# One level of Strassen's recursion on one row chunk in four of the gate and up projections

## The chip, the cores and the metric

The kernel runs on one NeuronCore of a Trainium2 chip. The core has a matrix engine (TensorE, PE in the profile), a vector engine (VectorE, DVE), a scalar engine (ScalarE, ACT), GpSimd (POOL) and a queue engine that issues loads (SyncE, SP). They run at the same time, each through its own list of instructions in order, and meet through semaphores. SBUF is the working memory with 128 partitions; PSUM holds eight banks of 128 x 512 fp32 numbers that only TensorE's products fill. The metric is the device time of one execution in microseconds.

## The reference

Two transformer blocks follow each other: one with an RWKV-7 branch and a softmax branch and a gated feed-forward part, and one with two kinds of attention. The change touches the feed-forward part of the first:

```python
    gate, up = jnp.split(_rms(h, n2) @ w_gu, 2, axis=-1)
    return h + (jax.nn.silu(gate) * up) @ w_dn
```

`h` has 256 rows that matter (plus 16 that are dropped at the end), the model width is 2048, and `gate` and `up` have 5632 columns each. So `w_gu` is a matrix of 2048 x 11264, all in fp32.

## The kernel before

**Precision by halves.** The products are made in the format fp32r, and each operand is split in two halves for it: `split` (lines 219 to 221) makes `hi` on ScalarE, a cast, and `lo = x - hi` on VectorE. `mm3` (line 270) multiplies with three matmuls, `hi hi + hi lo + lo hi`, into one PSUM bank.

**A weight chunk** is 256 rows by 512 columns of a matrix, held as 128 x 1024 numbers, 512 KB. `wload` (line 225) takes a raw buffer (three called `raw`, three called `raw2`, in turn), issues the load on SP's queue, and splits it into `hi` and `lo`, of which there are three buffers each. It does so with a raised priority, so that the order of the instructions has the loads and splits of later chunks ahead of the other work.

**A projection.** `gemm_b` (line 286) multiplies the 256 rows of activations by a column of chunks. Two banks of the four called `g` gather the two halves of the rows (`t` 0 and 1); for each chunk there are 2 x 2 x 3 = 12 matmuls, 128 x 512 each.

**The feed-forward stage** (lines 1008 to 1042). The 5632 hidden columns are 11 blocks of 512, in two groups (6 and 5). In each block `n`, `gemm_b` makes the gate from 8 chunks; ScalarE takes `tanh` of it (line 1028) and VectorE works on it (line 1029), both straight from the banks; `gemm_b` makes `up` from 8 more chunks, and VectorE multiplies (line 1032). Then `nat_to_t` (line 928) transposes the 256 x 512 result on TensorE, through the banks called `q` and `f`, and splits it into `hi` and `lo` for the next product. After each group the product with `w_dn` follows. A block has 16 chunks, 192 matmuls and 8 transposes.

**What sets the order.** From this stage on, a scheduler orders the instructions of all engines when the program is built, from the priorities and its own estimate of the times. On the chip each engine goes through its list as it stands: an instruction that waits holds back all that stands behind it on that engine, ready or not.

The functions that the change touches, with the line numbers of the profile:

## Time and profile before

| | |
|---|---|
| three runs | 2029.84, 2032.22 (median), 2036.05 us |
| the profiled execution | 2035.52 us, span 2033.8 us from its first to its last instruction |
| granted TensorE clock, mean | 0.989 |
| loads of `w_gu` | 176, of 512 KB each |
| matmul 128 x 512, in the feed-forward stage | 390 ns each in the records, which overlap |
| VectorE `lo` 128 x 1024, ScalarE `hi` 128 x 1024 there | 1225 ns, 1053 ns |

The two times differ by what lies around the span (1.7 us). In the rows below, a group of instructions reads: line, engine, operation, output<-input, shapes, count, then busy time and the mean of one in ns, then the idle time of the engine just ahead of them and what ended it. Rows of single instructions begin with the start and the length in microseconds; in brackets is the idle time ahead of it and what ended that. Rows that begin with A:B are stretches of the span: their length, then the busy time and the count of PE, PEld (TensorE's loads of the operand that stays in place), DVE, ACT and POOL, then the granted clock, the DMA engines' busy share, and GB/s.

### The profile page before, as it was taken

The numbers are of one execution on the slowest core, as the hardware profiler recorded it, in microseconds if no ns is written. First come the engines' busy times: TensorE is split into PE (matmuls) and PEld (weight loads), VectorE is DVE, ScalarE is ACT, GpSimd is POOL, SyncE is SP. The second block draws the span as 40 slices with busy tenths as digits, with TensorE's granted clock in tenths as the row PEclk, the third lists the DMA queues.
The fourth block names the chain that finished last, engine by engine and source line by source line (L and its number), as shares of the span: only waits on it lengthen the run. The fifth ranks groups of instructions, "written<-read, shape, count | busy, mean of one in ns | idle before, by whom it ended". The sixth has DMA issues, their size and how long they took to land.

```text
span 2033.8 us, 29647 instructions
## 1 busy us (share of the span) xinstructions
PE 1981.4 (97%) x11410; PEld 1698.3 (84%) x11410; DVE 1223.3 (60%) x2188; ACT 954.3 (47%) x1290; POOL 152.6 (8%) x226
## 2 busy tenths in 40 slices
PE   8998989999999999999999999999999999999998
PEld 7997879879767778888888888888888889998886
DVE  6787767778755456555555544555555655656555
ACT  6545445546444434554444433444444565444443
POOL 3131041221310000000000000000000000000000
PEclk9999999999999999999999999999999999999999
DMA  6644354444456676555555555555555565444564
GB/s 210 188 131 135 113 162 139 149 152 156 127 157 224 219 265 239 187 187 192 190 186 188 194 189 194 196 187 186 190 193 186 178 205 190 146 135 156 186 193 143
DMA packets 119566, 363.27 MB, mean 179 GB/s; under 512 B 28848, under 2 KB 29648, under 8 KB 119424
## 3 DMA queue, kind: packets, MB, share of 16 engines
q1 hardware_dynamic: 114576, 345.40, 51.7%
q0 software_dynamic: 4848, 15.97, 2.7%
q8 instruction: 89, 1.46, 0.3%
q14 instruction: 53, 0.43, 0.1%
HBM read 351.72 MB, written 9.60 MB: 178 GB/s over the span
## 4 chain that ended last, share of the span: by engine, by line
PE 86%; DVE 6%; DMA 4%; ACT 2%; issue 1%; POOL 1%; SPq 0%; DVEq 0%; ACTq 0%
PE g L263 78%; PE f L263 3%; DVE lo L221 3%; PE q L263 3%; DMA raw<-in_w_b 1%; PE f L267 1%; ACT hi L220 1%; PE q L267 1%; DVE xx L658 1%; DMA raw<-in_w_a 1%; POOL p L854 1%; DVE c L655 1%; DMA raw<-in_w_g 0%; DMA x<-in_xT 0%; DVE gt L589 0%
## 5 line engine op out<-in xcount | busy, mean ns | idle before, releaser
L221 DVE TENSOR_TENSOR lo<-raw,hi 128x1024 fp32r<-128x1024 f32 (+1 forms) x635 | 772.9, 1218 | 604.4 <-ACT hi L220 599.9
L263 PE MATMUL g<-hi,X 128*128 128x512 f32 (+1 forms) x3344 | 1045.5, 391 | 4.3 <-ACT X L220 1.7
L220 ACT CAST hi<-raw 128x1024 fp32r<-128x1024 f32 (+1 forms) x635 | 661.4, 1042 | 817.5 <-PE g L263 679.9
L263 PEld LDWEIGHTS g<-hi,X 128*128 128x128 f32 x3344 | 626.7, 188 | 135.0 <-issue 3.1
L263 PE MATMUL g<-lo,X 128*128 128x512 f32 (+1 forms) x1672 | 652.9, 391 | 2.7 <-DVE lo L221 2.7
L263 PE MATMUL g<-X,hi 128*128 128x272 f32 (+3 forms) x2176 | 430.3, 296 | 3.3 <-ACT hi L220 3.1
L263 PEld LDWEIGHTS g<-lo,X 128*128 128x128 f32 x1672 | 314.3, 188 | 67.5 <-DVE lo L221 5.1
L263 PEld LDWEIGHTS g<-X,hi 128*128 128x128 f32 (+1 forms) x2176 | 347.1, 193 | 10.7 <-ACT hi L220 3.6
L263 PE MATMUL g<-X,lo 128*128 128x272 f32 (+3 forms) x1088 | 318.2, 292 | 1.5 <-DVE lo L221 1.4
L263 PEld LDWEIGHTS g<-X,lo 128*128 128x128 f32 (+1 forms) x1088 | 209.4, 192 | 2.8 <-DVE lo L221 2.4
L263 PE MATMUL g<-hi,Y 128*128 128x512 f32 x544 | 171.0, 391 | 0.0
L263 PEld LDWEIGHTS g<-hi,Y 128*128 128x128 f32 x544 | 102.2, 188 | 20.7
L263 PE MATMUL g<-lo,Y 128*128 128x512 f32 x272 | 106.7, 392 | 0.0
L1049 POOL DMA_DIRECT2D cst<-in_cst x1 | 0.5, 541 | 832.6 <-DMA raw<-in_w_cq 832.6
L263 PEld LDWEIGHTS g<-lo,Y 128*128 128x128 f32 x272 | 51.1, 188 | 10.3
L854 POOL TENSOR_SCALAR p<-ckb,cq,qs 128x144 f32<-128x144 f32 (+1 forms) x32 | 45.6, 1434 | 66.2 <-DVE c L655 28.3
L655 DVE TENSOR_TENSOR c<-hq,xx 108x42 f32<-108x42 f32 (+31 forms) x236 | 40.3, 204 | 9.7 <-DMA hq<-hd 9.4
L658 DVE TENSOR_TENSOR xx<-xx,c 108x42 f32<-108x42 f32 (+31 forms) x236 | 40.8, 203 | 0.4
L420 POOL TENSOR_TENSOR d<-z 128x272 f32<-128x272 f32 (+3 forms) x28 | 22.4, 800 | 86.8 <-DVE z L419 56.0
L870 ACT ACTIVATE p<-p,fst,qs 128x144 f32<-128x144 f32 (+1 forms) x32 | 17.7, 553 | 7.8 <-DVE fst L869 7.6
L267 PE MATMUL f<-ident,p 128*128 128x128 f32 (+1 forms) x64 | 14.5, 333 | 6.6 <-DVE p L873 4.0
L1028 ACT ACTIVATE th<-g,r2h 128x512 f32<-128x512 f32 x22 | 15.1, 685 | 9.9 <-PE g L263 9.9
(425 smaller groups left out, 1342.9 us busy)
## 6 DMA issues: line engine op xcount, KB each, us to landing
raw<-in_w_gu SPq DMA_DIRECT2D x176, 512.0 KB
raw<-in_w_A SPq DMA_DIRECT2D x98, 512.0 KB
raw<-in_w_dn SPq DMA_DIRECT2D x88, 512.0 KB
raw<-in_w_g SPq DMA_DIRECT2D x64, 512.0 KB
raw<-in_w_o SPq DMA_DIRECT2D x32, 512.0 KB
raw<-in_w_qk SPq DMA_DIRECT2D x32, 512.0 KB
raw<-in_w_out SPq DMA_DIRECT2D x32, 512.0 KB
raw<-in_w_b SPq DMA_DIRECT2D x16, 512.0 KB
```

What stands on the lines that cost most here:

```text
L220: S.copy(hi, src)
L221: V.tensor_tensor(out=lo, in0=src, in1=hi.bitcast(F32), op=ALU.subtract)
L263: P.matmul(o, l, r, start=start, stop=stop, **k)
L267: P.transpose(o, i, eye)
L420: G.tensor_tensor(out=d[:m, t1:], in0=z[:m, t1:L], in1=z[:m, 1 + t1:], op=ALU.subtract)
L655: V.tensor_tensor(out=t_, in0=hs[:108, j, j + 1:].unsqueeze(1).to_broadcast([108, k_, w]), in1=xs[:, :, j:j + 1].to_broadcast([108, k_, w] ...
L658: V.tensor_tensor(out=xs[:, :, j + 1:], in0=xs[:, :, j + 1:], in1=t_, op=ALU.add)
L854: G.tensor_scalar(out=m_, in0=ckb[:, 2 * j + e, :n], scalar1=cq[:, t, hg:hg + 1], scalar2=qs[:, 0, t, 2 * j + e:2 * j + e + 1], op0=ALU.su ...
L870: S.activation(m_, m_, AF.Exp, bias=st[:, 1, sidx:sidx + 1], scale=qs[:, 1, t, h:h + 1], accum_out=st[:, 2, sidx:sidx + 1])
L1028: S.activation(th[:, t], pgt[t], AF.Tanh, scale=r2h[:, t:t + 1])
L1049: G.dma_start(cst2, a["cst2"])
```

## The change

Write the product of a pair of row chunks as a 2 x 2 block product: the left factor has two halves of rows (`t`) and two column chunks (`c` and `c + 4`), the right one the gate and up chunks that belong to them. Eight block products give the four blocks of the result. One level of Strassen's recursion, in the form with shared partial sums, makes them from seven products of sums and differences, and puts the results together with additions. The change does this for the pair (1, 5) of the four pairs (0, 4), (1, 5), (2, 6), (3, 7); the other three are multiplied as before.

Gate and up of a block are now made together by `gemm_s`, and their sums live in eight banks: m1, m6, m7, m5 in the four `g` banks, m2 and m3 in the two `q` banks, m4 and m8 in the two `f` banks. For the pair (1, 5), the raw chunks are b11 (gate 1), b21 (gate 5), b12 (up 1) and b22 (up 5). VectorE makes four differences from them (lines 356 to 359 of the changed kernel), and seven operands are split by `split`. b12 and b11 get raw buffers of their own, two called `raw3`. The sums of the activations for this pair are made once for all blocks, by `sums_x` on GpSimd. After the last of the seven products, ScalarE copies m1 (line 370) and VectorE makes four additions (lines 371 to 374); at the end of a block VectorE adds m2, m4, m3 and m8 (line 383). `tanh` and the products with it (lines 1115 to 1117) now read SBUF. The transposes of the hidden rows go through one `f` bank, and `th` and `junk` have one buffer in place of two.

```diff
@@ -298,6 +298,89 @@
             return [p[:, :n] for p in ps]
         ch = lambda w, g, c0, c1: [w[g, c] for c in range(c0, c1)]
+        def raw_w(src, p=None):
+            if p is None:
+                more_raw[1] = not more_raw[1]
+                p, n, b = (wp, "raw", 3) if more_raw[1] else (more_raw[0], "raw2", 3)
+            else:
+                n, b = "raw3", 2
+            raw = T(p, [128, 1024], n, bufs=b)
+            latest[0] = nc.sync.dma_start(raw.rearrange("p (n m) -> p n m", m=512), src)
+            return raw
+        def halves_w(raw):
+            hi, lo = (T(wp, [128, 1024], k, F32R, bufs=3) for k in ("hi", "lo"))
+            split(raw, hi, lo)
+            return tuple(t.rearrange("p (n m) -> p n m", m=512) for t in (hi, lo))
+        def sums_x(hi, lo, c, h, p, dst):
+            af = T(p, [128, 2, 2, 256], "T", bufs=3)
+            for k in range(2):
+                ks = slice(2 * (c + k * h), 2 * (c + k * h) + 2)
+                G.tensor_tensor(out=af[:, k], in0=hi[:, ks].bitcast(F32), in1=lo[:, ks].bitcast(F32), op=ALU.add)
+            blk = lambda t, k: af[:, k, :, 128 * t:128 * t + 128]
+            sf = T(p, [128, 4, 2, 128], "T", bufs=3)
+            G.tensor_tensor(out=sf[:, 0], in0=blk(1, 0), in1=blk(1, 1), op=ALU.add)
+            G.tensor_tensor(out=sf[:, 1], in0=sf[:, 0], in1=blk(0, 0), op=ALU.subtract)
+            G.tensor_tensor(out=sf[:, 2], in0=blk(0, 0), in1=blk(1, 0), op=ALU.subtract)
+            G.tensor_tensor(out=sf[:, 3], in0=blk(0, 1), in1=sf[:, 1], op=ALU.subtract)
+            split(sf, dst[0], dst[1])
+        def gemm_s(c1, c2, hi, lo, sx, p, e0, e1):
+            h = len(c1) // 2
+            m1, m6, m7, m5 = (bank("g") for _ in range(4))
+            m2, m3, m4, m8 = bank("q"), bank("q"), bank("f"), bank("f")
+            used = set()
+            def prod(ps, l, r, stop=False):
+                for j in range(2):
+                    mm3(ps, [v[:, j] for v in l], [v[:, j] for v in r], id(ps) not in used, stop and j == 1)
+                    used.add(id(ps))
+            blk = lambda t, c: [v[:, 2 * c:2 * c + 2, 128 * t:128 * t + 128] for v in (hi, lo)]
+            last = max(c for c in range(h) if c in sx)
+            for c in range(h):
+                end = c == h - 1
+                if c in sx:
+                    with tc.high_priority(offset=AHEAD):
+                        b12, b11, b22, b21 = (raw_w(v, q_) for v, q_ in ((c2[c], p), (c1[c], p), (c2[c + h], None), (c1[c + h], None)))
+                        t1, t2, t4 = (T(p, [128, 1024], "T", bufs=3) for _ in range(3))
+                        V.tensor_tensor(out=t1, in0=b12, in1=b11, op=ALU.subtract)
+                        V.tensor_tensor(out=b12, in0=b22, in1=b12, op=ALU.subtract)
+                        V.tensor_tensor(out=t2, in0=b22, in1=t1, op=ALU.subtract)
+                        V.tensor_tensor(out=t4, in0=b21, in1=t2, op=ALU.subtract)
+                    s_ = [[v[:, k] for v in sx[c]] for k in range(4)]
+                    stop = c == last
+                    for ps, l, r, st in (
+                        (m1, blk(0, c), b11, stop), (m2, blk(0, c + h), b21, False), (m3, s_[3], b22, False),
+                        (m5, s_[0], t1, stop), (m7, s_[2], b12, stop), (m6, s_[1], t2, stop), (m4, blk(1, c + h), t4, False),
+                    ):
+                        with tc.high_priority(offset=AHEAD):
+                            r = halves_w(r)
+                        prod(ps, l, r, st)
+                    if stop:
+                        S.copy(e0[:, 0], m1)
+                        V.tensor_tensor(out=e0[:, 1], in0=m6, in1=e0[:, 0], op=ALU.add)
+                        V.tensor_tensor(out=e1[:, 0], in0=m5, in1=e0[:, 1], op=ALU.add)
+                        V.tensor_tensor(out=e0[:, 1], in0=m7, in1=e0[:, 1], op=ALU.add)
+                        V.tensor_tensor(out=e1[:, 1], in0=m5, in1=e0[:, 1], op=ALU.add)
+                    continue
+                for src, k, ps in ((c1[c], c, (m2, m4)), (c1[c + h], c + h, (m2, m4)), (c2[c], c, (m3, m8)), (c2[c + h], c + h, (m3, m8))):
+                    r = wload(src, 2, 512)
+                    for t in range(2):
+                        prod(ps[t], blk(t, k), r, end and k >= h)
+                    if end and k >= h:
+                        e_ = e0 if ps[0] is m2 else e1
+                        for t in range(2):
+                            V.tensor_tensor(out=e_[:, t], in0=ps[t], in1=e_[:, t], op=ALU.add)
         vec = T(cp, [128, NVEC], "vec")
@@ -925,12 +1008,12 @@
             flip[0] ^= 1
             return bank("qf"[flip[0]])
-        def nat_to_t(src, hi, lo, kt0, gain=None):
-            n = src.shape[2] // 128
+        def nat_to_t(src, hi, lo, kt0, gain=None, ps=None):
+            n, one = src.shape[2] // 128, ps
             for k in range(0, n, 2):
                 m = min(2, n - k)
-                ps = bank2()
+                ps = bank2() if one is None else one
                 for j in range(m):
                     for t in range(2):
                         o = 256 * j + 128 * t
@@ -986,7 +1069,7 @@
                 for t in range(2):
                     V.tensor_tensor(out=hn[:, t, sl], in0=ps[t], in1=hn[:, t, sl], op=ALU.add)
                     if stat is not None:
-                        junk = T(p, [128, 512], "junk")
+                        junk = T(p, [128, 512], "junk", bufs=1)
                         S.activation(junk, hn[:, t, sl], AF.Square, accum_out=stat[:, t, n:n + 1])
             def rstd(stat, tag, n):
@@ -1015,23 +1098,25 @@
             units = (("X2", yp), ("X3", yp), ("Y0", yp), ("Y1", yp), ("X2", yp), ("X3", yp))
             ui = 0
             fgh, fgl = gh, gl
+            sx = {}
+            for c in (1,):
+                sx[c] = tuple(T(fp, [128, 4, 2, 128], f"S{c}", F32R, bufs=2) for _ in range(2))
+                sums_x(fgh, fgl, c, 4, fp, sx[c])
             for p0, p1 in ((0, 6), (6, 11)):
                 hid = []
                 for n in range(p0, p1):
                     if (n - p0) % 2 == 0:
                         hid.append(T(units[ui][1], [128, 2, 8, 256], units[ui][0], F32R))
                         ui += 1
-                    xg = lambda kt: (fgh[:, kt], fgl[:, kt])
-                    pgt = gemm_b(ch(a["w_gu"], n, 0, 8), xg)
-                    th = T(fp, [128, 2, 512], "th")
+                    e0, e1 = T(fp, [128, 2, 512], "e0", bufs=1), T(wp, [128, 2, 512], "gate", bufs=1)
+                    gemm_s(ch(a["w_gu"], n, 0, 8), ch(a["w_gu"], 11 + n, 0, 8), fgh, fgl, sx, fp, e0, e1)
+                    th = T(fp, [128, 2, 512], "th", bufs=1)
                     for t in range(2):
-                        S.activation(th[:, t], pgt[t], AF.Tanh, scale=r2h[:, t:t + 1])
-                        V.scalar_tensor_tensor(out=th[:, t], in0=th[:, t], scalar=1.0, in1=pgt[t], op0=ALU.add, op1=ALU.mult)
-                    pup = gemm_b(ch(a["w_gu"], 11 + n, 0, 8), xg)
-                    for t in range(2):
-                        V.scalar_tensor_tensor(out=th[:, t], in0=pup[t], scalar=r2s[:, t:t + 1], in1=th[:, t], op0=ALU.mult, op1=ALU.mult)
+                        S.activation(th[:, t], e0[:, t], AF.Tanh, scale=r2h[:, t:t + 1])
+                        V.scalar_tensor_tensor(out=th[:, t], in0=th[:, t], scalar=1.0, in1=e0[:, t], op0=ALU.add, op1=ALU.mult)
+                        V.scalar_tensor_tensor(out=th[:, t], in0=e1[:, t], scalar=r2s[:, t:t + 1], in1=th[:, t], op0=ALU.mult, op1=ALU.mult)
                     hu = hid[-1]
-                    nat_to_t(th, hu[:, 0], hu[:, 1], 4 * ((n - p0) % 2))
+                    nat_to_t(th, hu[:, 0], hu[:, 1], 4 * ((n - p0) % 2), ps=bank("f"))
                 last = p1 == 11
                 if last:
                     gh, gl = unit("X0", xp), unit("X1", xp)
```

The order of the instructions, at the two places that the prediction speaks of. In the names, `X0` and `X1` are the halves of the activations, `S1` those of their sums, and a number tells one use of a buffer from another. The first place is VectorE where a block ends and the next begins. Before, around the last two operations of the first block (`lo_9431` is gate 1 of the next block, `lo_9449` gate 2 and so on, `g_9247` and `g_9248` are the banks of the old block's `up`, `X2` the hidden rows' halves):

```order
L221 TENSOR_TENSOR lo_9431<-raw_9429,hi_9430 128x1024 [waits DMAHW2_49,Activation_49]
L1032 SCALAR_TENSOR_TENSOR th_9242<-g_9247,r2s_9091,th_9242 128x512 [waits PE_49]
L1032 SCALAR_TENSOR_TENSOR th_9242<-g_9248,r2s_9091,th_9242 128x512 [waits PE_49]
L221 TENSOR_TENSOR lo_9449<-raw2_9447,hi_9448 128x1024 [waits DMAHW3_49,Activation_49]
L221 TENSOR_TENSOR lo_9467<-raw_9465,hi_9466 128x1024 [waits DMAHW4_49,Activation_49]
L221 TENSOR_TENSOR X2_9095<-f_9395,X2_9095 128x512 [waits Activation_49]
L221 TENSOR_TENSOR X2_9095<-q_9402,X2_9095 128x512 [waits Activation_49]
L221 TENSOR_TENSOR lo_9485<-raw2_9483,hi_9484 128x1024 [waits DMAHW5_49,Activation_49]
L221 TENSOR_TENSOR lo_9503<-raw_9501,hi_9502 128x1024 [waits DMAHW6_49,Activation_49]
```

Now, behind the `lo` of the first block's last chunk (`lo_9460` and `lo_9478` are chunks gate 0 and gate 4 of the next block, `lo_9496` is its up 0; `q_9114` is m2, `f_9116` m4, `q_9115` m3, `f_9117` m8 of the old block):

```order
L383 TENSOR_TENSOR e0_9108<-q_9114,e0_9108 128x512 [waits PE_49]
L357 TENSOR_TENSOR raw3_9530<-raw2_9534,raw3_9530 128x1024 [waits DMAHW7_49]
L358 TENSOR_TENSOR T_9539<-raw2_9534,T_9538 128x1024
L383 TENSOR_TENSOR e0_9108<-f_9116,e0_9108 128x512 [waits PE_49]
L221 TENSOR_TENSOR lo_9460<-raw2_9458,hi_9459 128x1024 [waits DMAHW3_49,Activation_49]
L1116 SCALAR_TENSOR_TENSOR th_9428<-th_9428,e0_9108 128x512 [waits Activation_49]
L359 TENSOR_TENSOR T_9540<-raw_9536,T_9539 128x1024 [waits DMAHW0_49,DVE_49]
L221 TENSOR_TENSOR lo_9478<-raw_9476,hi_9477 128x1024 [waits DMAHW4_49,Activation_49]
L383 TENSOR_TENSOR gate_9109<-q_9115,gate_9109 128x512 [waits PE_49]
L1116 SCALAR_TENSOR_TENSOR th_9428<-th_9428,e0_9108 128x512 [waits Activation_49]
L383 TENSOR_TENSOR gate_9109<-f_9117,gate_9109 128x512 [waits PE_49]
L221 TENSOR_TENSOR lo_9496<-raw2_9494,hi_9495 128x1024 [waits DMAHW5_49,Activation_49]
```

Between two `lo`s stood at most two operations of the block's end; now three differences, four additions and two products stand among three `lo`s, and `lo_9496` stands behind the addition that waits for the block's last matmul (`f_9117`).

The second place is TensorE some 40 matmuls into a block. Before, where a chunk of the next block begins (`g_9409` and `g_9410` are the gate's banks):

```order
L263 MATMUL g_9410<-hi_9430,X1_8401 128x512
L263 MATMUL g_9409<-hi_9448,X0_8400 128x512 [waits Activation_49]
L263 MATMUL g_9409<-lo_9449,X0_8400 128x512 [waits DVE_49]
L263 MATMUL g_9409<-hi_9448,X1_8401 128x512
L263 MATMUL g_9410<-hi_9448,X0_8400 128x512
L263 MATMUL g_9410<-lo_9449,X0_8400 128x512
```

Now, at the second half of the transposes (`th`), the product of b21 (`hi_9555`) and the second product of up 0 (`hi_9495`, into m8):

```order
L267 MATMUL f_9435<-ident_76,th_9428 128x128 [waits DVE_49]
L267 MATMUL f_9435<-ident_76,th_9428 128x128 x3
L263 MATMUL q_9454<-hi_9555,X0_8400 128x512 [waits Activation_49]
L263 MATMUL q_9454<-lo_9556,X0_8400 128x512 [waits DVE_49]
L263 MATMUL q_9454<-hi_9555,X1_8401 128x512
L263 MATMUL q_9454<-hi_9555,X0_8400 128x512
L263 MATMUL q_9454<-lo_9556,X0_8400 128x512
L263 MATMUL q_9454<-hi_9555,X1_8401 128x512
L263 MATMUL f_9457<-hi_9495,X0_8400 128x512 [waits DVE_49]
```

Before, both products of a chunk stood together. Now the halves of up 0, `hi_9495`, were used for m3 ahead of the transposes and are used again behind them and behind b21's product, and the same holds for up 4.

## The prediction

> **What bounds the kernel now.** I read the page first, then the stage that the change touches in stretches of one block (one pass of the loop over `n`, 512 hidden columns), then single instructions there.
>
> ```profile
> PE 1981.4 (97%) x11410; PEld 1698.3 (84%) x11410; DVE 1223.3 (60%) x2188; ACT 954.3 (47%) x1290; POOL 152.6 (8%) x226
> PE 86%; DVE 6%; DMA 4%; ACT 2%; issue 1%; POOL 1%; SPq 0%; DVEq 0%; ACTq 0%
> 903.00:947.00 44.00, 44.00 (x200) 36.49 (x199) 23.08 (x23) 19.07 (x21) 0.00 (x0) 1.00 0.58 188
> 947.00:991.00 44.00, 44.00 (x200) 36.51 (x199) 23.06 (x23) 19.07 (x20) 0.00 (x0) 1.00 0.57 187
> ```
>
> The first two rows are shares over the whole span. The other two decide: in a block TensorE works 44.00 us of 44.00 (the columns after the length are PE, PEld, DVE, ACT, POOL), at a granted clock of 1.00. A matmul saved there shortens the time, and a wait on TensorE lengthens it by all of itself. VectorE works 23.1 us of 44.0.
>
> ```profile
> 901.83 28.11 PE g L263 x124
> 929.94 0.11 PE f L267
> 936.99 1.05 ACT L220 CAST hi<-raw 128x1024 fp32r<-128x1024 f32 x1 [1.67 <-PE g L263]
> 939.71 1.05 ACT L220 CAST hi<-raw 128x1024 fp32r<-128x1024 f32 x1 [1.66 <-PE g L263]
> ```
>
> In the chain of waits 124 matmuls take 28.11 us, 0.227 each, and a transpose 0.11. A weight chunk feeds 12 matmuls, 2.72 us, and that is the distance of the two casts. Each cast waits for TensorE: it wants one of three `hi` buffers, so it starts when the chunk three before has left. The kernel already runs as far ahead as these buffers let it.
>
> **The change part by part.**
>
> *Saved.* A pass of the recursion does with 7 products of 6 matmuls what took 8, so a block has 186 matmuls for 192. Over 11 blocks that is 66 x 0.227 = 15.0 us, all on TensorE's full path.
>
> *Added on VectorE, per block.* Three more `lo` halves and four differences, 128x1024; eight additions of products, 128x512.
>
> ```profile
> L221 DVE TENSOR_TENSOR lo<-raw,hi 128x1024 fp32r<-128x1024 f32 x80 | 98.0, 1225 | 96.4 <-ACT hi L220 95.8
> 948.96 1.23 DVE L221 TENSOR_TENSOR lo<-raw,hi 128x1024 fp32r<-128x1024 f32 x1 [0.35 <-ACT hi L220]
> 950.10 0.68 DVE L1029 SCALAR_TENSOR_TENSOR th<-th,g 128x512 f32<-128x512 f32 x1
> 931.37 0.69 DVE L221 TENSOR_TENSOR X<-f,X 128x512 fp32r<-128x512 f32 x1 [1.14 <-ACT X L220]
> 931.98 0.68 DVE L221 TENSOR_TENSOR X<-q,X 128x512 fp32r<-128x512 f32 x1
> 903.68 1.04 ACT L220 CAST hi<-raw 128x1024 fp32r<-128x1024 f32 x1
> 904.62 0.69 ACT L1028 ACTIVATE th<-g,r2h 128x512 f32<-128x512 f32 x1
> ```
>
> From start to start a wide VectorE operation occupies 948.96 to 950.10 = 1.14 us (its result is there after 1.23), a half-wide one 931.37 to 931.98 = 0.61, a cast 903.68 to 904.62 = 0.94 (result after 1.05). So VectorE gets 7 x 1.14 + 8 x 0.61 = 12.9 us more, about 36 in a block of 44.1 - 1.4 = 42.7. ScalarE gets three casts and a copy, 3.4 us on 19. As averages both fit beside TensorE. That is why I don't stop there: VectorE works in order, and where these 15 operations stand decides.
>
> *What follows on TensorE at a block's end.* Before, `gemm_b` took two of four `g` banks in turn, and a block's end asked VectorE for two operations. Now the eight products of a block hold all eight banks, and by the order of the instructions VectorE does, between the `lo` of a block's last chunk and the `lo` of the next block's third chunk (u0, up 0): an addition (m2), the differences of L357 and L358, an addition (m4), `lo` of g0, one of L1116, the difference of L359, `lo` of g4, an addition (m3), L1116, an addition (m8), `lo` of u0. I walk it with the durations above; time 0 is the end of the old block's last matmul. A result is taken up about 0.05 after it is there:
>
> ```profile
> 945.15 1.05 ACT L220 CAST hi<-raw 128x1024 fp32r<-128x1024 f32 x1 [1.66 <-PE g L263]
> 946.23 1.23 DVE L221 TENSOR_TENSOR lo<-raw,hi 128x1024 fp32r<-128x1024 f32 x1 [1.49 <-ACT hi L220]
> 946.76 0.62 PE L263 MATMUL g<-hi,X 128*128 128x512 f32 x2
> 947.19 0.69 ACT L1028 ACTIVATE th<-g,r2h 128x512 f32<-128x512 f32 x1 [0.99 <-PE g L263]
> ```
>
> (A cast's 945.15 + 1.05 = 946.20 is followed at 946.23; a matmul's last result comes 0.39 after its start, 0.16 after the next may start.) The landing of a weight chunk, 512 KB, is priced from the stage where the chain runs through it:
>
> ```profile
> 685.36 3.40 DMA raw<-in_w_b
> 691.20 3.69 DMA raw<-in_w_b
> 697.30 6.67 DMA raw<-in_w_b
> ```
>
> 3.40 to 3.69 with little else in flight, 6.67 with two others. I take 3.6, since a block asks for 16 chunks in 42 us and the queue now waits for its buffers. [...]
>
> - The last chunk's cast starts when its buffer is free, at -8.16 + 0.2 = -7.95; its `lo` is done at -5.7.
> - The addition to m2 ends at -5.1. L357 needs b22 (u5), whose raw buffer came free with the `lo` of the chunk before, -8.4; it lands at -4.8. L357, L358, the m4 addition, `lo` of g0, L1116 and L359 end at -3.65, -2.5, -1.9, -0.75, -0.15, 1.0; `lo` of g4 is there at 2.25. TensorE has done g0 (6 matmuls) and one of g4 at 1.6. **Stop 1: 0.7.**
> - Three half-wide operations, then `lo` of u0, from 4.0 to 5.2. TensorE is there at 3.7. **Stop 2: 1.5.**
> - Now 12 matmuls into m4 and four transposes, to 9.55. u0's halves stay occupied, because its second product (m8) needs a bank that the transposes and VectorE still hold. u4's cast gets g0's buffer at 8.05, b11's gets g4's at 9.4 and is done at 10.45. **Stop 3: 0.7.**
> - u0 and u4 hold two of the three buffers, so b21 must wait until b11's product is finished, 13.2. Its cast ends at 14.25, TensorE had come to it at 13.45; its `lo` ends at 15.5, TensorE wants it at 14.55. **Stops 4 and 5: 0.8 and 1.0.**
> - The other products follow at 1.36 us each, and VectorE's 1.14 keeps up. Then L356 for the next block stands ahead of `lo` of g2. It needs b11, loaded into the raw buffer that m7's operand leaves at 22.3; landed at 25.9, L356 done at 27.1, `lo` at 28.3; TensorE wanted it at 27.0. **Stop 6: 1.3.**
>
> Together 6.0 us a boundary. There are 5 + 4 = 9 such boundaries (each of the two groups of blocks ends in `w_dn`, whose products use the free `g` banks; the last boundary lacks stop 6). The first block has no predecessor but the norm's last transposes: between 0 and 6, I take 5, since it has the same seven products on three buffers. Sum of the stops 9 x 6.0 - 1.3 + 5 = 57.7. After a stop the first matmuls are slower too:
>
> ```profile
> 697.33 0.50 PE L263 MATMUL g<-lo,X 128*128 128x512 f32 x1 [0.48 <-DVE lo L221]
> 697.66 0.40 PE L263 MATMUL g<-hi,X 128*128 128x512 f32 x1
> ```
>
> 0.33 from start to start in place of 0.227, so 0.1 for each of some 55 stops, 5.5. **The sum: 57.7 + 5.5 - 15.0 = +48 us.** The profiled execution has a span of 2033.8 and a time of 2035.52, so it would take 2083.7; the median of the runs lies 3.3 below it, which gives 2080.4.
>
> *Edits at nothing.* `sums_x` (six operations on GpSimd, a split) runs once, on column tiles that the norm finished some 20 us earlier; POOL's whole work in a block is 0.00 us, and TensorE reaches the first use some 10 us into block 0. If it were late, it costs its own length once:
>
> ```profile
> L564 POOL TENSOR_TENSOR t<-t 128x512 f32<-128x512 f32 x4 | 8.9, 2234 | 60.7 <-DVE x L550 33.3 <-DVE x L552 27.4
> L420 POOL TENSOR_TENSOR d<-z 128x256 f32<-128x256 f32 x10 | 7.5, 754 | 25.1 <-DVE z L418 14.5 <-DVE z L419 8.6 <-DVE c L655 1.7
> ```
>
> 2 x 2.2 + 4 x 0.75 = 7.5 us. One buffer instead of two for `th` and `junk`: the next `th` is written 40 us later. The number of loads is unchanged.
>
> *Bounds.* From below: a quarter off each stop (57.7 x 0.75 - 15, no slower restart) leaves +28, 2060. From above: two waits a boundary hang on a landing (L357, L356), 18 in all; at 6.67 they add 18 x 3.1 = 55, 2136; at a mean of 5.0, 18 x 1.4 = 25, 2106.
>
> **The rivals.**
>
> *Late loads* (2095 to 2136). The same boundary, with landings of 4.5 to 6.7. For it: the row of 6.67. Against it: in blocks DMA share is 0.57, in that stage 0.75.
>
> *The gain comes through* (2017; the other side). The stops are absorbed: VectorE has 6 us of idle time a block even after the change, and if the lead that the buffers give covers the 15 operations, only 15 us less remain, 2032.2 - 15.0. It decides where a boundary costs under 15.0 / 9 = 1.7 us. For it: the averages. Against it: the lead is one chunk, 2.7 us, and the list between two `lo`s is over 10 us of work with 7 us of matmuls ahead of it.
>
> *Only VectorE's queue binds* (2032.2 + 9 x 2.2 - 15 = 2037). Stops 1 and 2 come, 3 to 6 don't, if casts find buffers sooner. Against it: the cadence of 2.72 above shows casts waiting for TensorE in every chunk.
>
> *The clock falls* (about 2165). If the stops made TensorE lose its clock, the 42 matmuls between stops 1 and 5 at half rate cost 42 x 0.227 = 9.5 more, 9 times 86. Against it is a stage with just such stops, at a clock of 1.00:
>
> ```profile
> 685.00:760.00 75.00, 68.69 (x293) 53.86 (x292) 41.07 (x42) 30.48 (x30) 3.72 (x7) 1.00 0.75 244
> ```
>
> [...] The row shows 6.3 us idle in 75 and no swing, so I leave 2 in 100.
>
> *It doesn't do what it says.* The instruction list has 66 matmuls fewer, so this would need stops of just 15 us, chance.
>
> **How the numbers follow.** Forecast 0.78; late loads 0.12; gain 0.05; queue alone 0.02; clock 0.02; a draw 0.01. I put the time at 2082, within a microsecond or two of the sum, because loads can only be later than 3.6, hardly sooner. The range 2060 to 2108 holds the forecast with its lower bound and landings up to 5.0. What can be told from no change is about 0.3%, 6 us: faster 0.05, same 0.02, slower 0.93.
>
> **What would show it.** In a block of the new profile TensorE's busy share should fall to about 43 of 49 us, with idle time on `lo` and `hi` (six places a boundary, 0.7 to 1.5 each), and VectorE at about 36 of 49. Blocks should last 42.7 + 6.0 + 0.6 = 49 us against 44.1. L356 or L357 should show waits for a load. Wrong would be: blocks of 42.7 us (the gain came through), stops only on `lo` of g4 and u0, waits on loads of several us, or a granted clock under 0.95.

## The result, and the profile after

| | before | after |
|---|---|---|
| median of four runs | 2033.15 us | 2091.81 us |
| the profiled execution's span | 2033.8 us | 2092.6 us |
| matmuls | 11410 | 11344 |

The change makes the kernel slower by 58.7 us: ratio 1.0284, 95% interval 1.0256 to 1.0313. The forecast was 2082, within 2060 to 2108. What follows asks where the ten microseconds beyond the forecast come from, and which of the six stops hang together.

The page of the changed kernel, the busy times and the chain of waits by engine:

```profile
PE 1991.1 (95%) x11344; PEld 1683.3 (80%) x11344; DVE 1363.4 (65%) x2354; ACT 996.6 (48%) x1335; POOL 161.4 (8%) x232
PE 72%; DVE 13%; DMA 7%; ACT 4%; issue 3%; POOL 1%; SPq 0%; DVEq 0%; ACTq 0%
```

TensorE has fallen from 86 to 72% of the chain; VectorE has gone from 6 to 13, loads from 4 to 7. The stage in stretches of one block (length, then PE, PEld, DVE, ACT, POOL, the granted clock, DMA share, GB/s):

```profile
977.00:1027.00 50.00, 45.13 (x196) 35.45 (x196) 36.15 (x38) 22.84 (x25) 0.00 (x0) 1.00 0.51 168
1077.00:1130.00 53.00, 46.79 (x196) 36.66 (x196) 36.30 (x38) 22.90 (x26) 0.00 (x0) 0.97 0.49 160
```

TensorE is now idle for about 5 us in each block, and two blocks of nine are 3 us longer still, with a clock below 1.00. From one block's first `tanh` to the next the distance is 49.7 to 49.9 us, in two cases 52.8 and 52.9, and 48.4 and 48.5 at the first and the last; in the kernel before it is 44.43 (the 44.1 of the prediction was the first block, which is shorter). The first instructions after idle time on TensorE at one boundary, start, length, and in brackets the idle time and what ended it:

```profile
1083.65 0.50 PE L263 MATMUL q<-lo,X 128*128 128x512 f32 x1 [0.55 <-DVE lo L221]
1086.59 0.50 PE L263 MATMUL q<-lo,X 128*128 128x512 f32 x1 [1.26 <-DVE lo L221]
1092.03 0.50 PE L263 MATMUL g<-hi,X 128*128 128x512 f32 x1 [0.58 <-ACT hi L220]
1095.99 0.50 PE L263 MATMUL q<-hi,X 128*128 128x512 f32 x1 [0.70 <-ACT hi L220]
1097.25 0.50 PE L263 MATMUL q<-lo,X 128*128 128x512 f32 x1 [0.76 <-DVE lo L221]
1111.10 0.50 PE L263 MATMUL q<-lo,X 128*128 128x512 f32 x1 [2.37 <-DVE lo L221]
```

These are the six stops. The rows count idle time from a modelled end, 0.39 after a matmul's start, while the next could have started after 0.227; so each stop is 0.16 longer than its bracket: 0.7, 1.4, 0.7, 0.9, 0.9, 2.5. Their brackets hardly vary from boundary to boundary (stop 1 was once 1.16), but for the sixth, which goes from 0.90 to 2.37. The waits of the whole stage (engine and line, what it waited for: us in total, times, longest), first TensorE's, then VectorE's for loads:

```profile
PE q L263 <- DVE lo L221: 35.5, 36, 2.4
PE q L263 <- ACT hi L220: 6.3, 9, 0.7
PE g L263 <- ACT hi L220: 5.2, 9, 0.6
DVE T L356 <- DMA raw<-in_w_gu: 9.2, 10, 2.0
DVE raw L357 <- DMA raw<-in_w_gu: 4.1, 10, 1.0
```

And the pieces of the chain of waits in which a load is on it, at an ordinary boundary and at the long one (start, length):

```profile
1053.96 3.47 DMA raw<-in_w_gu
...
1103.78 4.88 DMA raw<-in_w_gu
```

### The profile page after: what moved, and what is told of

It reads as the page before. It is cut to its first block, busy times and chain, and to the rows that moved or that the text cites. A ratio compares the mean times of both kernels' runs of the same rounds, so it can differ in the third digit from the quotient of the medians.

```text
span 2092.6 us, 29747 instructions
## 1 busy us (share of the span) xinstructions
PE 1991.1 (95%) x11344; PEld 1683.3 (80%) x11344; DVE 1363.4 (65%) x2354; ACT 996.6 (48%) x1335; POOL 161.4 (8%) x232
## 4 chain that ended last, share of the span: by engine, by line
PE 72%; DVE 13%; DMA 7%; ACT 4%; issue 3%; POOL 1%; SPq 0%; DVEq 0%; ACTq 0%
PE g L263 53%; PE f L263 9%; PE q L263 8%; DVE lo L221 6%; DMA raw<-in_w_gu 3%; ACT hi L220 3%; DMA raw<-in_w_b 1%; PE f L267 1%; PE q L267 1%; DVE xx L741 1%; DVE c L738 1%; POOL p L937 1%; DMA raw<-in_w_a 1%; DVE T L358 1%; DVE gate L383 1%
## 5 line engine op out<-in xcount | busy, mean ns | idle before, releaser
L263 PE MATMUL g<-hi,X 128*128 128x512 f32 (+1 forms) x1980 | 626.0, 392 | 11.2 <-ACT hi L220 8.4
L263 PEld LDWEIGHTS g<-hi,X 128*128 128x128 f32 x1980 | 370.7, 188 | 92.6 <-ACT hi L220 12.1
L263 PE MATMUL g<-lo,X 128*128 128x512 f32 (+1 forms) x990 | 386.9, 391 | 3.3 <-DVE lo L221 3.2
L263 PEld LDWEIGHTS g<-X,hi 128*128 128x128 f32 (+1 forms) x2176 | 346.0, 192 | 11.6 <-ACT hi L220 4.3
L263 PEld LDWEIGHTS g<-lo,X 128*128 128x128 f32 x990 | 186.3, 188 | 43.5 <-DVE lo L221 7.2
L263 PE MATMUL q<-hi,X 128*128 128x512 f32 x572 | 199.8, 396 | 6.5 <-ACT hi L220 6.3
L263 PE MATMUL f<-hi,X 128*128 128x512 f32 x572 | 198.5, 396 | 0.2 <-DVE X L1028 0.2
L263 PE MATMUL q<-lo,X 128*128 128x512 f32 x286 | 115.6, 404 | 35.5 <-DVE lo L221 35.5
L263 PEld LDWEIGHTS q<-hi,X 128*128 128x128 f32 x572 | 108.0, 189 | 30.2 <-ACT hi L220 8.4
L263 PEld LDWEIGHTS f<-hi,X 128*128 128x128 f32 x572 | 108.4, 190 | 25.7 <-ACT hi L220 2.1
L263 PE MATMUL f<-lo,X 128*128 128x512 f32 x286 | 112.0, 392 | 0.0
```

The source lines that it names most:

```text
L263: P.matmul(o, l, r, start=start, stop=stop, **k)
```

## The experiments

Each kernel is the changed one with the edit shown. Differences are against the median of the kernel before on the same chip. The period is the usual distance between two blocks.

| kernel | median, us | against before | ratio, 95% interval | period |
|---|---|---|---|---|
| the change | 2091.8 | +58.7 | 1.0256 to 1.0313 | 49.7 |
| differences left out | 2040.2 | +7.2 | 1.0013 to 1.0041 | 45.24 |
| own buffers for u0, u4 | 2044.6 | +11.6 | 1.0035 to 1.0069 | 45.3 |
| both | 2021.7 | -13.5 | 0.9914 to 0.9949 | 43.1 |
| differences on GpSimd | 2101.6 | +68.6 | 1.0311 to 1.0350 | 51.4 |
| on GpSimd, and own buffers | 2100.1 | +67.0 | 1.0277 to 1.0346 | 50.6 |
| no recursion, eight banks | 2055.0 | +21.8 | 1.0075 to 1.0121 | 46.30 |
| no recursion, own buffers | 2037.0 | +2.6 | 1.0001 to 1.0022 | 44.6 |
| four buffers for b11, b12 | 2081.4 | +48.1 | 1.0215 to 1.0257 | 48.8 to 49.6 |
| the pair (2, 6) | 2060.4 | +26.0 | 1.0110 to 1.0146 | 46.8 |
| the pair (0, 4) | 2034.0 | +0.8 | 0.9988 to 1.0018 | 43.13 |
| the pair (0, 4), not in block 0 | 2025.8 | -7.4 | 0.9951 to 0.9980 | 43.16 |

In the texts written ahead, the "order theory" is that of the prediction: stops 1, 2 and 6 come from VectorE's list, 3 to 5 from u0 and u4, which hold two of the three `hi`/`lo` buffers. Its rivals: the sheer work of VectorE, the eight banks that tie two blocks together, late loads.

### The differences left out

```diff
-   t1, t2, t4 = (T(p, [128, 1024], "T", bufs=3) for _ in range(3))
-   V.tensor_tensor(out=t1, in0=b12, in1=b11, op=ALU.subtract)
-   ... (L357 to L359)
+   t1, t2, t4 = b12, b22, b21
```

> Left out: the four differences of each block (lines 356 to 359); the raw chunks b12, b22 and b21 go into the products of t1, t2 and t4 as they are, so gate and up are other numbers. All loads, halves, matmuls, additions and banks stay. Order theory (the stops come where VectorE's list stands ahead of a `lo`, and where u0 and u4 hold two of three buffers): four operations of 1.14 us fall out of the list at the boundary; stop 6 goes, because no operation that waits for b11's load stands ahead of the `lo` of g2 any more; stops 1 and 2 (0.55 and 1.26 us idle in the rows) go, because 3.4 us of differences stood ahead of them; stop 3 goes if it was only the echo of stops 1 and 2; stops 4 and 5 (0.70 and 0.76) stay, because u0 and u4 still hold their buffers. So 1.46 + 2 x 0.26 (modelled ends, restart) = 2.0 us a boundary, 9 x 2.0 = 18, less the 15.0 saved: +3, with the first block's share about +4, 2037 us (2032 to 2045), blocks of 45. Work theory (what counts is how much VectorE and ScalarE have to do): 4.6 of the 12.9 us of new VectorE work go, so a third of the 73 us of loss, about 2066. Bank theory (the eight banks tie the end of one block to the start of the next): nothing changes at the transposes, 2080 or more. Load theory: the loads are the same, the casts now wait for them where the differences did, 2070 to 2090.

2040.2. TensorE's waits in this stage:

```profile
PE q L263 <- DVE lo L221: 6.8, 9, 0.8
PE q L263 <- ACT hi L220: 6.3, 9, 0.7
```

Nine times the pair 0.70 and 0.76, stops 4 and 5, and nothing else: stops 1, 2, 3 and 6 are gone with 4.6 of the 12.9 us of new VectorE work. A theory of the sheer work, which gives a third of the loss back, misses by 26 us.

### Buffers of their own for u0 and u4

```diff
- r = wload(src, 2, 512)
+ r = wload(src, 2, 512, dst=(ex[:, 2 * (k // h)], ex[:, 2 * (k // h) + 1]) if c == 0 and ps[0] is m3 else None)
  # ex: T(yp, [128, 4, 1024], "Y1" if n < 6 else "Y0", F32R), one per block
```

> The halves of u0 and u4 (up 0 and up 4) go into buffers of their own in a 16 KB unit that is unused at the time, so that they no longer hold two of the three; VectorE's operations are the same in number and kind. Order theory: stops 3, 4 and 5 go (0.58, 0.70, 0.76 idle), and all later casts come two buffers sooner; stops 1 and 2 stay (0.55 and 1.26), stop 6 stays if the load of b11 is late by itself (0.9 to 2.4) and goes if only the held buffers made it late. So 1.8 + 0.5 = 2.3 us a boundary, 21 in all, less 15.0: +6, 2039 us; with stop 6, 11 more: 2050. Work theory: no work is taken away, so 2085 or more. Bank theory: 2080 or more. Load theory: the loads' buffers come free sooner with the casts, so perhaps half of the loss goes, 2060.

2044.6. Here VectorE does everything that it does in the change. The stops at one boundary (at others the first is 0.12 to 1.05 idle):

```profile
1063.32 0.50 PE L263 MATMUL q<-lo,X 128*128 128x512 f32 x1 [0.84 <-DVE lo L221]
1066.20 0.50 PE L263 MATMUL q<-lo,X 128*128 128x512 f32 x1 [0.99 <-DVE lo L221]
```

Two stops on `lo` in VectorE's list stay, 3 to 5 are gone, and so is the sixth, although L356 still waits for its load (here in the first group of blocks):

```profile
DVE T L356 <- DMA raw<-in_w_gu: 5.5, 5, 1.2
```

So a late load was not enough for stop 6: it became a stop because the casts behind it had no lead. The load theory had said 2060, two thirds of this gain.

### Both at once

> Both relieved at once without GpSimd: u0 and u4 in buffers of their own, and the four differences left out (the raw chunks b12, b22, b21 go into the products as they are, so gate and up are other numbers). This is the fourth corner of a square: the change 2091.8, differences out 2040.2, buffers of their own 2044.6. Order theory: the stops that are left in the one (4 and 5) and in the other (1 and 2) are different ones, so none is left; blocks of 43.1, the saving less 2 to 3 us of the start: 2021 us (2016 to 2028). If the two were the same microseconds counted twice, the time would not fall below the better of the two, 2038 to 2042. If what spoiled the run with the differences on GpSimd and own buffers (2100) was not GpSimd but the pair of edits, it shows here too: 2060 to 2100.

2021.7, blocks without a stop:

```profile
977.00:1020.00 43.00, 43.00 (x195) 35.41 (x194) 31.27 (x33) 22.41 (x24) 0.00 (x0) 1.00 0.60 195
```

The two stops that each edit alone leaves are different ones, and together they leave none. But the edits are not additive: by the differences from before, they are worth 51.5 and 47.1 us alone and 72.2 together. Stops 3 and 6 need both, a list on VectorE that is late and buffers that are held, and either edit removes them. The eight banks, the additions and the loads are here as in the change, and make no stop by themselves.

### The differences on GpSimd, without and with own buffers

```diff
- V.tensor_tensor(out=t1, in0=b12, in1=b11, op=ALU.subtract)
+ G.tensor_tensor(out=t1, in0=b12, in1=b11, op=ALU.subtract)
  (and so the other three)
```

> The four differences go to GpSimd, nothing else is changed, the result is the same. A half-wide operation takes 2.23 us there in the profile before, so a wide one some 4.5 and the four some 18 of a block's 45 us, in a row that starts when b11 is there, some 15 us before the products need it. Order theory: as with the differences left out, +4, 2037 us (2032 to 2045), because only their place in VectorE's list cost anything; if GpSimd is late for t1 (m5's operand), one more stop of up to 4 us a boundary, 2070. Work theory in a form that counts memory traffic: the same traffic lies on SBUF, VectorE's operations get longer than 1.22 us beside GpSimd's, and the time is between 2040 and 2066. Bank or load theory: 2080 or more.

> Both edits together: the differences on GpSimd and buffers of their own for u0 and u4. Order theory: no stop is left, and the 66 matmuls saved come through: 2033 - 15 = 2018 us (2014 to 2025), 0.7% faster than before, blocks of 43. If each stop had a cause of its own (no coupling), the two edits would also be right in sum. Work theory: as with the differences on GpSimd alone, 2040 to 2066. Bank theory: 2080 or more, since the eight banks and the eight additions are the same. If GpSimd is late for t1 in blocks that are now shorter, 2030 to 2060 with stops on the cast or `lo` of T.

2101.6 and 2100.1: the order theory missed by 64 and 82 us. The work theory in its second form had named what happens, that VectorE's operations get longer beside GpSimd's, but priced it at 2066 at most. The "2080 or more" of the bank and load theories was reached, but not for their reasons: the kernel with both edits has the same banks and loads and no stop. GpSimd was faster than I had priced it (2.4 to 3.4 us an operation, for 4.5); it made VectorE slow. VectorE and GpSimd in the kernel with own buffers, rows of two lists:

```profile
980.64 1.21 DVE L221 TENSOR_TENSOR lo<-raw,hi 128x1024 fp32r<-128x1024 f32 x1
981.77 0.68 DVE L383 TENSOR_TENSOR e<-f,e 128x512 f32<-128x512 f32 x1
982.37 2.83 DVE L221 TENSOR_TENSOR lo<-raw,hi 128x1024 fp32r<-128x1024 f32 x1
985.12 5.61 DVE L1116 SCALAR_TENSOR_TENSOR th<-th,e 128x512 f32<-128x512 f32 x2
990.66 1.21 DVE L221 TENSOR_TENSOR lo<-raw,hi 128x1024 fp32r<-128x1024 f32 x1
...
959.81 2.39 POOL L356 TENSOR_TENSOR T<-raw,raw 128x1024 f32<-128x1024 f32 x1 [20.48 <-DMA raw<-in_w_gu]
980.95 3.17 POOL L357 TENSOR_TENSOR raw<-raw,raw 128x1024 f32<-128x1024 f32 x1 [18.75 <-DMA raw<-in_w_gu]
984.07 3.37 POOL L358 TENSOR_TENSOR T<-raw,T 128x1024 f32<-128x1024 f32 x1
987.52 2.67 POOL L359 TENSOR_TENSOR T<-raw,T 128x1024 f32<-128x1024 f32 x1
```

Alone, GpSimd's operation takes 2.39 us and VectorE's 1.21. Side by side both lengthen: the `lo` that starts at 982.37 ends at 985.2, 1.1 after L357's end (984.12); L358 ends at 987.44, 2.24 after that `lo`; the two L1116, 1.3 us of work, end at 990.73, after L359 (990.19). VectorE's L383, which reads one of its operands from PSUM, takes its usual 0.68 while L357 runs. Through what the two lengthen each other is not shown. With the differences on GpSimd alone TensorE then waits 4.28 us for one `lo` at each of the nine boundaries, and its clock falls to 0.50 at each; with own buffers it waits 2.87 to 5.01 us, and the clock falls at eight of the nine (mean granted clock of the two traces 0.981 and 0.975, of the change 0.986). A stop and the clock in stretches, with the differences on GpSimd alone:

```profile
933.10 0.80 PE L263 MATMUL q<-lo,X 128*128 128x512 f32 x1 [4.28 <-DVE lo L221]
```

```profile
930.00:932.00 2.00, 0.00 (x0) 0.00 (x0) 2.00 (x1) 0.00 (x0) 1.96 (x1) 0.81 0.00 0
...
936.00:938.00 2.00, 2.00 (x7) 1.62 (x6) 0.70 (x1) 0.00 (x0) 0.00 (x0) 0.50 0.16 35
```

### No recursion, in the order of the change

```diff
- for c in (1,):
+ for c in ():
- V.tensor_tensor(out=e_[:, t], in0=ps[t], in1=e_[:, t], op=ALU.add)
+ V.tensor_copy(e_[:, t], ps[t])
```

> No recursion: all four pairs are multiplied in the ordinary way (192 matmuls a block), but gate and up together, in the eight banks of the change, with u0 and u4 as early as there; at a block's end VectorE copies m2, m4, m3, m8 to SBUF, where the change adds them. So the new order of the block alone, with no difference and no sum; the result is the same. Order theory: only the stops that come from u0 and u4 holding two of three buffers: 4 and 5, 0.70 + 0.76 idle, 2.0 a boundary with restarts; 9 x 2.0 = 18 and perhaps a little in the first block, nothing saved: 2033 + 18 = 2051 us (2045 to 2058), blocks of 46.4. If the stops come from the work of the recursion, with VectorE now at some 30 us a block, no stop at all: 2033. Bank theory: all of the loss is here, 2033 + 73 = 2106 without the saving, at least 2090.

2055.0, near the far end of the order theory's 2045 to 2058. With no difference, no sum and 25.6 us of VectorE's work a block (the text had said some 30), two stops remain:

```profile
PE q L263 <- ACT hi L220: 6.3, 9, 0.7
PE q L263 <- DVE lo L221: 4.7, 9, 0.5
```

The new order of a block alone, gate and up together in eight banks, costs 21.8 us. That part of the loss has nothing to do with Strassen's recursion. Its cause was tested by giving u0 and u4 own buffers here too:

> No recursion, gate and up together in the eight banks, and u0 and u4 in buffers of their own (the unused 16 KB unit). The result is the same. Against the kernel without recursion in the eight banks alone, this takes away only what holds two of the three `hi`/`lo` buffers. If those held buffers make its two stops (0.70 and 0.53 idle, blocks of 46.3, 2055 us), both go and blocks are 44.4 to 44.5 as before the change: 2035 us (2031 to 2040). If the stops come from the banks (the transposes and the copies that hold m8's bank), blocks stay at 46.3 and the time at 2055.

2037.0, and for the whole stage one wait:

```profile
PE q L263 <- DVE lo L221: 0.2, 1, 0.2
```

The held buffers make those stops, and the eight banks cost next to nothing by themselves.

### Four raw buffers for b11 and b12

```diff
  (shortened; for b11 and b12 alone)
- raw = T(p, [128, 1024], "raw3", bufs=2)
+ rb_[1] = (rb_[1] + 1) % 4
+ raw = rb_[0][:, rb_[1]]     # rb_[0]: T(yp, [128, 4, 1024], "Y0" if p0 else "Y1"), one per group
```

> The change as it is, except that the raw chunks b11 and b12 have four buffers in turn in place of two (in a unit of 16 KB that is unused at the time), so that b11 of the next block is loaded a block ahead and L356 waits for no load. This takes away stop 6 and nothing else at its place. In the rows of the change stop 6 came to 0.90, 1.04, 0.95, 2.37, 1.00, 1.88, 0.98, 1.23 = 10.4 us, with restarts 12.4; and if the two longest are what made the clock fall twice, another 3.4: 2092 - 16 = 2076 us (2072 to 2084), granted clock without a fall in this stage. If the clock falls for another reason, it falls here too and the time is 2080. If L356 is late for VectorE's own list and not for its load, nothing changes: 2090.

2081.4. No stop of the sixth kind is left, and no fall of the clock after the first block; the gain is 10.4 of the 16 us expected. Part of the rest is stop 1, which became longer at some boundaries (up to 1.22 idle, 1.9 us more in nine rows): now L357 waits more for b22 (its line is L362 here). The other parts are a fall of the clock in block 0, after a stop of 3.79 us there (1.7 us lost), and three new stops in the first block of the second group (1.2 us idle).

```profile
DVE Y L362 <- DMA raw<-in_w_gu: 5.4, 9, 1.2
```

### Another pair

```diff
- for c in (1,):
+ for c in (2,):      # and (0,) in the next
```

> The recursion on the pair (2, 6) in place of (1, 5): now the pair is third of four in a block, its chunks are loaded and their differences made in the middle of the block, away from the boundary; u0 and u4 come first as in the kernel without recursion, so two buffers stay held. The result is the same. Order theory: stops 1, 2 and 6 go with the differences; the two stops of the held buffers stay, 0.70 + 0.53 idle as without recursion or up to stops 4 and 5 with 0.76, so 1.8 to 2.0 a boundary with restarts; whether the seven operands at 1.36 us each are still in time behind a held buffer is open, 0 to 2 us a block more: 2033 - 15 + 9 x 1.9 = 2035, up to 2055 us. If the eight banks, the work or the loads set the loss and not the place of the pair, 2080 or more, as with the pair (1, 5).

2060.4, beyond the 2055 that I had named as the far end. I had assumed that the differences move to the middle of the block. They did not: L357 to L359 stand 13 to 17 us behind the boundary's first addition, and L356 ahead of the boundary. VectorE's list, and the stop that comes of it:

```profile
1025.45 1.23 DVE L221 TENSOR_TENSOR lo<-raw,hi 128x1024 fp32r<-128x1024 f32 x1 [1.60 <-ACT hi L220]
1027.41 1.23 DVE L357 TENSOR_TENSOR raw<-raw,raw 128x1024 f32<-128x1024 f32 x1 [0.74 <-DMA raw<-in_w_gu]
1028.56 1.22 DVE L358 TENSOR_TENSOR T<-raw,T 128x1024 f32<-128x1024 f32 x1
1029.69 1.22 DVE L221 TENSOR_TENSOR lo<-raw,hi 128x1024 fp32r<-128x1024 f32 x1
```

```profile
1030.96 0.50 PE L263 MATMUL q<-lo,X 128*128 128x512 f32 x1 [2.01 <-DVE lo L221]
```

The cast of that `lo` was done at 1026.7. L357 stood ahead of it, waiting for a load, and L358 behind L357; 3 us in the list, 2.0 on TensorE. It is the mechanism of stop 6 at a new place, once a block.

> The recursion is applied to the pair of row chunks (0, 4) in place of (1, 5): the same number of matmuls, halves, differences, additions, loads and buffers, the result is the same. Now the pair comes first in a block and u0 and u4 no longer exist as chunks with two products each ahead of it. Order theory: the raw chunks of the pair are the first loads of a block, so they land in the block before, where VectorE has pauses of 1.5 us between `lo`s, and the differences go there; the seven products that come first need one bank each, and their halves leave at once, so no buffer is held across the transposes. Stops 1 to 6 all go: block about 44.4 - 1.4 = 43.1, less the start, where block 0 still has no lead (5.3 us idle in the rows of the first block of the change, with restarts 7): 2033 - 15 + 7 = 2025 us, range 2018 to 2040. Work theory: as much work as before, 2085 or more. Bank theory: 2080 or more. Load theory (the chunks of the pair are simply late): stops of 1 to 2 us on a load once a block, 2030 to 2050.

2034.0: the same work and the same buffers as in the change, 58 us less. The period is 43.13 us, and in a block there is no stop:

```profile
970.00:1013.10 43.10, 43.10 (x195) 35.68 (x194) 35.48 (x38) 22.59 (x25) 0.00 (x0) 1.00 0.59 195
```

VectorE has its 35.5 us a block here as there. What the saving gives, the start of block 0 takes:

```profile
882.58 0.79 PE L263 MATMUL g<-hi,X 128*128 128x512 f32 x1 [6.42 <-ACT hi L220]
```

with a clock of 0.50 from about 878 to 888. Without the recursion in block 0:

```diff
- gemm_s(..., fgh, fgl, sx, fp, e0, e1)
+ gemm_s(..., fgh, fgl, sx if n else {}, fp, e0, e1)
  (and in block 0 VectorE copies m2, m4, m3, m8 where it adds them elsewhere)
```

> As the kernel with the pair (0, 4), but block 0 is multiplied without the recursion (6 matmuls more, 1.4 us), so that its sums of activations have a whole block's time. Order theory: the first block's stops of about 7 us go with them, so some 5 to 6 us less than with the recursion in all blocks, 2020 us (2015 to 2033). If the first block's stops come from the eight banks rather than from the sums and differences, the same time as with the recursion in all blocks, or 1.4 us more.

2025.8, the fastest kernel here that computes everything: 0.9966 of the time before, interval 0.9951 to 0.9980. Where its differences stand, VectorE's list of one block:

```profile
997.53 1.23 DVE L221 TENSOR_TENSOR lo<-raw,hi 128x1024 fp32r<-128x1024 f32 x1 [1.50 <-ACT hi L220]
1000.30 1.23 DVE L357 TENSOR_TENSOR raw<-raw,raw 128x1024 f32<-128x1024 f32 x1 [1.55 <-DMA raw<-in_w_gu]
1001.44 1.22 DVE L358 TENSOR_TENSOR T<-raw,T 128x1024 f32<-128x1024 f32 x1
1002.58 1.22 DVE L221 TENSOR_TENSOR lo<-raw,hi 128x1024 fp32r<-128x1024 f32 x1
```

L357 to L359 stand 9 to 6 us ahead of the boundary (the first addition of L383 is at 1009.55), and L356 still earlier, between `lo`s that have pauses of 1.5 us before them. L357 even waits longer for its load than in the change, and it costs nothing.

## Why the prediction was right, term by term

**The walk held.** At the boundary shown, the six stops were forecast as 0.7, 1.5, 0.7, 0.8, 1.0, 1.3 and came as 0.7, 1.4, 0.7, 0.9, 0.9 and 2.5. The sixth varies: its mean over eight boundaries is 1.45 (brackets of 0.90 to 2.37, plus 0.16). VectorE worked 36.15 us in a block of 50, as forecast 36 of 49.

| term | forecast, us | trace |
|---|---|---|
| matmuls saved | -15.0 | 11 x (44.43 - 43.16) = -14.0 |
| stops | 57.7 | 50.6 idle in 59 rows + 59 x 0.16 = 60.1 |
| slower restart | 5.5 | 59 x 0.11 = 6.5 |
| clock | 0 | 2 x 1.7 = 3.4 |
| sum | +48.2 | +56.0 |

(43.16 is the longer of the two periods with the pair (0, 4), where nothing stops within a block; with the other, 43.13, it is -14.3. A restart is 1063.32 to 1063.66, 0.34 for 0.227, in the rows of the kernel with own buffers.) From the last addition after `w_o` to the first after `w_dn` in the second group it is 881.7 to 1586.5 in the trace of the change and 880.3 to 1527.7 in that of before, 57.4 us longer; 1.4 us of it is not accounted for.

**What was mis-sized.** *Stop 6*, through the landing of b11: at an ordinary boundary the load's piece in the chain was 3.47 us (I had taken 3.6), but at two of the eight it was 4.40 and 4.88, and the stop 1.88 and 2.37. *The first block*: 5.3 us idle in six rows, 6.3 with the modelled ends, for 5. That it came so near is luck, since the reason given, the seven products on three buffers, is not what the two long rows show. The 2.63 ends at 891.62 with a cast of ScalarE that stands behind L1027, a copy of the norm's last transposes, which waits 1.54 us for VectorE; VectorE's `lo` ahead of that took 1.84 us in place of 1.23, while GpSimd made the sums of `sums_x`, which I had put at nothing. The 1.67 at 910.60 is stop 6 again: L356 waits 1.29 us for its load. *The saving*: 1.27 a block, not 1.36; no run here shows why. *The clock* was put at nothing in the sum. After each of the two longest stops 6 it fell, here after the 2.37:

```profile
1110.00:1112.00 2.00, 0.90 (x4) 0.78 (x5) 2.00 (x3) 0.00 (x0) 0.00 (x0) 1.00 0.00 0
1112.00:1114.00 2.00, 2.00 (x8) 1.52 (x7) 2.00 (x3) 0.00 (x0) 0.00 (x0) 0.62 0.75 258
1114.00:1116.00 2.00, 2.00 (x6) 1.58 (x5) 1.50 (x3) 1.05 (x1) 0.00 (x0) 0.53 0.91 217
```

2 x 0.38 + 2 x 0.47 = 1.7 us lost each time. That explains the two long blocks: 1.4 us more of stop 6 and 1.7 of clock, 49.7 + 3.1 = 52.8; in the other 0.9 of stop 6, 0.65 of the one long stop 1 (1.16 idle), and 1.7 of clock.

**The reasons.** That VectorE's list costs TensorE at stops 1, 2 and 6 is shown by leaving the differences out, and by the pair (0, 4), where the same list stands elsewhere. That u0 and u4 make stops 4 and 5 is shown by their own buffers, with the recursion and without. Stop 3 I had put down to a late cast of b11 by buffers alone; it goes with either edit, so it needs the stops ahead of it as well as the held buffers.

**The rivals.** *Late loads*: 2095 to 2136 was not reached, but the measured 2091.8 is nearer to it than to 2082. Of 18 loads in the stage's chain 14 took 3.42 to 3.76 us and four 4.19 to 4.88. The late ones made two stops 6 longer by 2.3 us and one stop 1 by 0.65, and the clock fell twice behind them, 3.4: some 6 of the 9 us that the stage lost beyond the sum. So the rival was true at a few boundaries. The sum had no term for it; the range, with landings up to 5.0, had room. *The gain comes through*: not in this order, but its reason, that the averages leave room, is true: with the pair (0, 4) it comes through in every block but the first. The prediction's argument against it, a list of over 10 us ahead of 7 us of matmuls, belongs to the order with the pair (1, 5); with (0, 4) TensorE waits for no such list. *Only VectorE's queue binds*: 2037 was forecast for stops 1 and 2 alone, and the kernel with own buffers, where only such stops are left, took 2044.6. *The clock falls*: not at every boundary and not for long, but the row that I held against it (6.3 us idle in 75, clock 1.00) was made of stops of 1.71 us at most, all shorter than the two that did it (1.88 and 2.37).

## What to carry to other kernels

Costing a change on an engine with idle time by its average shows only whether it can fit; what it costs is read from the list at the place where the consumer has the least lead, and moving the same operations to where the list has pauses (here, another pair) can be worth more than the change itself. Operands whose second use comes late take buffers from everything behind them: count how many of the buffers are held across a stage's boundary before anything is added there. GpSimd was no free hand beside VectorE here: a `lo` with both operands in SBUF took 2.83 us in place of 1.21 beside its differences, and a difference up to 3.37 in place of 2.39, so lengths of either taken alone did not give the time of the two side by side.

## What the runs showed of the hardware that I had not expected

**VectorE and GpSimd side by side.** 1.21 us became 2.83, and two operations of 1.3 us together became 5.6, beside GpSimd's differences. Ahead of these runs I had priced GpSimd's wide operation at twice a half-wide row of 2.23; a wide one alone took 2.39 here. The row of 2.23 was not of GpSimd alone either: each of those four operations (2.11 to 2.30) began beside a `lo` of VectorE of 1.22, and in the trace of the change two half-wide ones (the first of `sums_x`), beside no `lo`, take 2.55 together.

**The clock fell after pauses of 1.82 to 2.87 us.** Pauses of 1.88, 2.37 (the change), 2.87 (GpSimd with own buffers) and 1.82 (the pair (2, 6)) were followed by a clock of one half for 3.41 us; with one of 4.28 (above) it fell within the pause, for 6.83 us. Others as long were not followed by any fall: 2.63 in block 0 of the change, another of 2.87 in the kernel with GpSimd and own buffers, 2.99 with the pair (2, 6). In the traces of the change and of before, all falls begin a whole number of 3.413 us apart (in the change at 1112.48 and 1388.96, 81 of them). In the feed-forward stage a fall lasts one of them (3.41, the change), two (6.83, the differences on GpSimd) or three (about 878 to 888, the pair (0, 4)).

What fits these pauses is how much of one lies in a single such interval. The interval that ends in a fall of the change, the two over which its pause of 2.63 us is spread, and the one that ends in the fall with the pair (2, 6) (the second column is TensorE's busy time):

```profile
1109.07:1112.48 3.41, 1.38 (x6) 1.17 (x7) 3.41 (x4) 0.52 (x1) 0.00 (x0) 1.00 0.09 13
887.21:890.62 3.41, 1.78 (x11) 1.22 (x9) 3.38 (x5) 1.30 (x4) 3.25 (x5) 1.00 0.80 322
890.62:894.03 3.41, 2.20 (x9) 1.62 (x10) 3.41 (x5) 2.37 (x4) 1.35 (x1) 1.00 0.46 154
...
1122.66:1126.07 3.41, 1.59 (x8) 0.97 (x7) 3.41 (x5) 0.00 (x0) 0.00 (x0) 1.00 0.37 137
```

In this stage of the change's trace 205 such intervals began at full clock. The two in which TensorE was busy for 1.38 and 1.53 us ended in a fall; the others, from 1.73 us on, did not. That is a reading of this trace and of this stage alone: in its other stages, with other forms of matmul, the same busy time does not separate the two (intervals of up to 2.68 us ended in a fall, one of 1.70 did not). No run here varied a pause alone, so this is read from the traces and not tested.
